# Low parts of the q, k, v and o weights: formed by an adding GpSimd DMA instead of a VectorE subtraction

## The chip, the core and the metric

The kernel runs on one core of a Trainium2 chip. A core has five engines with their own instruction queues: TensorE (PE, the matrix products; PEld is its weight load), VectorE (DVE), ScalarE (ACT), GpSimd (POOL) and SyncE (SP, which here only issues DMAs). Each queue runs in order and waits on semaphores for the others. Data move between HBM and SBUF by 16 DMA engines. The metric is the device time of one execution in microseconds (us).

## The reference

The program is a decoder trunk on 512 tokens of 1024 channels: a layer that mixes tokens by causal average pooling and a small linear map per group, a layer of causal stick-breaking attention with 16 heads of 64, and a squared-ReLU MLP with 4096 hidden channels behind each. All have an RMS norm in front and behind. What matters here is the attention layer:

```python
def rms_norm(x, g):
    y = xf * lax.rsqrt(jnp.mean(xf * xf, axis=-1, keepdims=True) + EPS)
    return (y * g.astype(jnp.float32)).astype(x.dtype)
...
kv = jnp.matmul(rms_norm(x, kv_norm_g), w_kv).reshape(B, S, 2, N_HEADS, HEAD_DIM)
...
q = jnp.matmul(h, w_q[j]).reshape(B, S, N_HEADS, HEAD_DIM).transpose(0, 2, 1, 3)
o = stick_breaking_attention(q, k, v)
m = jnp.matmul(o.transpose(0, 2, 1, 3).reshape(B, S, HD), w_o[j])
```

In the attention, the weight of a key is sigmoid(z) times the product of sigmoid(-z) over the keys between it and the query, and zero for keys from the query on.

## The kernel before, in words

Activations and weights are float32. A product is made of three TensorE products in the faster float32r form: an operand is split into a high part (the value rounded to float32r) and a low part (the value less its high part), and high x high, high x low and low x high are added up in PSUM. `up_block` (L534 to L536) and `mm3` (L209 to L211) issue these triples.

A weight block is 128 x 1024, 512 KB. `weight` (L105 to L121) makes its two parts. SyncE loads the block into a `raw` tile, of which there are two. For v, k and q `gains` scales it in place by a norm's gain on GpSimd, in two halves (L130). ScalarE casts it into the high part `hi` (L118). VectorE subtracts `hi` from `raw` into the low part `lo` (L120). For four blocks of the first MLP GpSimd makes the subtraction (`ON_POOL`). The parts lie in four tiles each, and `fill` and `get` make up to four weights ahead of their use, in the order of a list. There are 32 such blocks in the attention: eight each of v (four units of two halves), k and q (one a pair of heads) and o (the output projection).

The attention runs through a list of steps, `ATT_ORDER`. V makes the values of a unit of four heads, for the token tiles listed; P the queries and keys of a pair of heads; S its weights; T their transposes (L759); A their products with the values (L769); O and E the output projection. In S, TensorE makes the scores (L721, L722), ScalarE two sigmoids (L727, L728), GpSimd sets the part above the diagonal by affine selections (L733, eight a head), VectorE runs a product scan (L740) and a last product (L743). S0 to S7 below are the S steps of the pairs 0 to 7.

The program is not issued in the order in which it is written. A planner with its own cost of each instruction orders the engines' queues; the waits between engines follow from the tiles that are read and written. `issue_after` holds the scaling, cast and subtraction of a weight behind named instructions of the same engine (`behind`), so that they don't get ahead of the softmax. Within a queue nothing overtakes.

Of the kernel before, what the change touches and what calls it, by code (L numbers as in the profile page):

```python
# [10 lines left out]
F32 = mybir.dt.float32  # L11
F32R = mybir.dt.float32r
ACT = mybir.ActivationFunctionType
ALU = mybir.AluOpType

P = 128
# [16 lines left out]
# Columns of the score tile of a head: query tiles 3, 2, 1, 0, each with the keys it may see.  # L33
SEG = {3: (0, 512), 2: (512, 384), 1: (896, 256), 0: (1152, 128)}
NSEG = 1280
# The order of the pooling mixer: norm of a token tile (s), pooling (p), linear map and residual (m),
# norm (n), transposes (t); F: the next weights.
# [4 lines left out]
# Weights whose low part GpSimd makes, while VectorE has the norms to do.  # L42
ON_POOL = {("up", 0, j) for j in (0, 1, 2, 4)}

# The order of the attention. V: values of four heads, for the token tiles listed; K: keys of two
# heads for the first two token tiles; P: queries and keys of two heads; S: their weights; T: the
# transposes of those; A: their products with the values; O: output projection of four heads, for the
# token tiles listed; E: of the last eight.
# [6 lines left out]
# Rows of the gains that go along the free axis.  # L55
R_MIX_POST0, R_MLP_POST0, R_MIX_POST1, R_MLP_POST1, R_SCALE, R_MLP_PRE0, R_MLP_PRE1 = range(7)
# Blocks of the gains that go along partitions.
# [4 lines left out]
def trunk(ctx, tc, x, consts, gcol, grow, pw, wup, wdn, wq, wk, wv, wo, out):  # L62
# [18 lines left out]
    # ---- loads that everything waits for  # L81
# [19 lines left out]
    # The last instructions of a part by engine: the scaling and splitting of weights that are traced  # L101
    # after them keep behind them; from the first scores on (gate), behind all such work traced before.
    behind, latest = {}, {}

    # ---- weights: loaded, scaled by a gain if asked, split into two float32r parts  # L105
    def weight(src, tiles, scaled=None, on=nc.vector):
        raw = wts.tile([P, D], F32, tag="raw", bufs=2, name=name("raw"))
        nc.sync.dma_start(raw, src)

        def later(engine):  # L110
            return tc.issue_after(behind[engine].ins) if engine in behind else nullcontext()

        if scaled is not None:
            with later("pool"):
                scaled(raw)
        hi, lo = tiles
        with later("act"):
            nc.scalar.copy(hi, raw)  # L118
        with later("dve"):
            on.tensor_tensor(out=lo, in0=raw, in1=hi.bitcast(F32), op=ALU.subtract)  # L120
        return hi, lo  # L121

    def gains(lo, n):
        """scales the n blocks of a weight by the gains along partitions from column lo"""

        def scaled(raw):
            v = raw.rearrange("p (k c) -> p k c", k=n)
            g = gc[:, lo : lo + n].rearrange("p (k o) -> p k o", o=1)
            for h in (slice(0, n // 2), slice(n // 2, n)):
                nc.gpsimd.tensor_tensor(  # L130
                    out=v[:, h], in0=v[:, h], in1=g[:, h].broadcast_to((P, n // 2, D // n)), op=ALU.mult
                )

        return scaled
# [6 lines left out]
    def place(k):  # L141
        """hi and lo tiles of a weight"""
        if k[0] == "dn":
            return [dn_pool[0].tile([P, D], F32R, tag="w", bufs=8, name=name(x)) for x in "hl"]
        if k == ("o", 6):
            both = att_pool[0].tile([P, 2, D], F32R, tag="v", bufs=2, name=name("w"))
            return [both[:, 0], both[:, 1]]
        if k == ("o", 7):
            return [att_pool[0].tile([P, NSEG], F32R, tag="u", bufs=2, name=name(x))[:, :D] for x in "hl"]
        return [wts.tile([P, D], F32R, tag=f"w{x}", bufs=4, name=name(x)) for x in "hl"]  # L150

    def make():
        k, src, scaled = queue.pop(0)
        on = nc.gpsimd if k in ON_POOL else nc.vector
        made[k] = weight(src, place(k), scaled, on)
# [30 lines left out]
    # ---- parts of a layer  # L186
# [7 lines left out]
    def rstd(st, col, eps=EPS, op=ALU.add, third=False):  # L194
        """1 / rms from the mean squares of two halves in columns col and col + 1 (and of a third part,
        in column col + 4), and eps"""
        total = st[:, col + 2 : col + 3]
        latest["dve"] = nc.vector.tensor_scalar(
            out=total, in0=st[:, col : col + 1], scalar1=st[:, col + 1 : col + 2],
            scalar2=eps, op0=ALU.add, op1=op,  # L200
        )
        if third:
            nc.vector.tensor_tensor(out=total, in0=total, in1=st[:, col + 4 : col + 5], op=ALU.add)
        r = st[:, col + 3 : col + 4]
        latest["pool"] = nc.gpsimd.tensor_tensor(out=r, in0=total, in1=mhalf, op=ALU.pow)
        return r
# [9 lines left out]
    # ---- x += rms_norm(y) * gain, and the norm (with its gain, if given) and the transposes of the new  # L216
    # x, token tile by token tile, in steps that are traced where the engines get to them
# [3 lines left out]
    class Update:  # L221
        def __init__(self, t, gpost, scaled, eps=EPS, gpre=None, final=False):
            self.t, self.gpost, self.scaled, self.eps = t, gpost, scaled, eps
            self.gpre, self.final = gpre, final
            self.xn = xn_tile()
            self.st = keep.tile([P, 8], F32, tag=f"stat{t}", bufs=4, name=name("stat"))
            # The last tile of all ends in smaller parts, for less to do behind the last product.
            self.cuts = [NS[0], slice(512, 768), slice(768, 1024)] if final and t == T - 1 else NS

        def square(self, n, y, on):  # L230
            """part n of y, and its product with the gain"""
            cut = self.cuts[n]
            square_sum(y, self.xn[:, cut], self.st, (0, 1, 4)[n])
            on.tensor_tensor(out=self.scaled[:, cut], in0=y, in1=self.gpost[:, cut], op=ALU.mult)
# [18 lines left out]
        def rstd(self):  # L253
# [3 lines left out]
            # The MLP is homogeneous: f(c x) = c^2 f(x). It gets x / sqrt(m), m the mean square, and so  # L257
            # gives y (m + EPS) / m, whose norm has EPS ((m + EPS) / m)^2 in place of EPS. Thus no
            # token is small beside those that the MLP's products add it to. m is kept from 0.
# [33 lines left out]
    def contract(lhs, w, y, first, update=None, tiles=range(T), soon=False):  # L293
        """y[t] (+)= lhs.T @ w, token tile by token tile; update(t, y[t]) makes what follows each, the
        transposes of the first tile before the products of the last if soon"""
# [66 lines left out]
    class Seven:  # L362
        """y += r.T @ w over two pairs of blocks by the seven products of Strassen's algorithm in
        Winograd's form. The halves of the tokens (of r) and of the columns (of w) and the two blocks of
        a pair make the parts r11 ... w22; the products are summed over the pairs on TensorE:

            y11 = r11 w11 + r12 w21         y12 = u + s1 t1 + s4 w22
            y21 = u + s3 t3 + r22 t4        y22 = u + s1 t1 + s3 t3        u = r11 w11 + s2 t2
            s1 = r21 + r22    s2 = s1 - r11    s3 = r11 - r21    s4 = r12 - s2
            t1 = w12 - w11    t3 = w22 - w12   t2 = t3 + w11     t4 = w21 - t2  # L370

        A sum in PSUM is added to y whenever it is one of these sums, and then goes on."""

        # Bank pair, operands, and the part of y that gets what the bank pair holds by then.
# [12 lines left out]
        def feed(self, r):  # L387
            """the left operands that the next block of r brings"""
# [23 lines left out]
        def prepare(self):  # L412
            """the right operands one by one, in the order of their use"""
# [32 lines left out]
        def make(self, n):  # L446
            """the next n right operands"""
# [29 lines left out]
    def mlp(l, mp, update):  # L477
        """The last group of blocks goes plainly, token tile by token tile, as the update wants y."""
# [59 lines left out]
    # ---- layer 0: pooling mixer  # L538
    with tc.tile_pool(name="mix0", bufs=1, reuse_waits="tile") as mp:
        # Products that keep TensorE busy until the data are there: its clock is gated while it idles  # L540
# [87 lines left out]
    # ---- layer 0: MLP  # L628
# [5 lines left out]
    # ---- layer 1: stick-breaking attention  # L634
    with tc.tile_pool(name="att", bufs=1, reuse_waits="tile") as ap:
# [25 lines left out]
        def start(key):  # L661
            """the projection of the first two token tiles"""
# [19 lines left out]
        # The low parts of the keys of a head, above or below zeros.  # L682
# [27 lines left out]
        def weights(qk, a):  # L710
            """The weights of head a of a pair: sigmoid(z) times the product, over the keys between
            the key and the query, of sigmoid(-z); none for keys from the query on."""
# [110 lines left out]
    # ---- layer 1: MLP  # L823
# [6 lines left out]
def constants():  # L830
    """The identity, and the pooling windows as band matrices (source token, target token): of the
    first token tile, of a later one, and of a tile and the one before it."""
# [47 lines left out]
```

## Time and profile before

| | |
|---|---|
| median of 3 runs (range) | 999.75 us (999.0 to 1001.27) |
| span of the profiled execution | 999.6 us; the profile gives no other time of it |
| TensorE busy | 957.3 us, 96% |
| VectorE, ScalarE, GpSimd busy | 785.3, 555.7, 315.8 us |
| mean granted clock of TensorE | 0.984 |
| attention | about 350 to 650 us |

In the profile a group of instructions has the line of the kernel, the engine, the operation, the tiles (out<-in, buffer numbers left out), the shapes and the count, then the busy time and the mean duration of one, and last the idle time of the engine just before them and what ended it. In a table of windows each engine has its busy time and in brackets the number of its instructions. In a timeline a row has start and duration, and in square brackets the idle time before it.

### The profile page before, as it was taken

How to read it: one execution, taken by the hardware profiler on the slowest of the kernel's cores; microseconds unless marked ns; L12 is line 12 of the kernel's file. 1: busy time of each engine (PE TensorE's matmuls, PEld its weight loads, DVE VectorE, ACT ScalarE, POOL GpSimd, SP SyncE). 2: the span in 40 equal slices, each digit the busy share in tenths (PEclk: the TensorE clock that was granted, in tenths of full speed). 3: DMA queues.
4: the chain of work that ended last, by engine and by line, in shares of the span. 5: the costliest groups of instructions: out<-in, count | busy, mean ns of one | idle time of the engine just before them, and what ended most of it. 6: DMA issues, size and time to landing. Idle time of an engine off the chain costs nothing.

```text
span 999.6 us, 13220 instructions
## 1 busy us (share of the span) xinstructions
PE 957.3 (96%) x4823; PEld 812.1 (81%) x4823; DVE 785.3 (79%) x1115; ACT 555.7 (56%) x989; POOL 315.8 (32%) x351
## 2 busy tenths in 40 slices
PE   7898999999999999989998999989999999999997
PEld 6896888888888888888787988788888888888886
DVE  5987788878878747578687999989778878888636
ACT  5666646456455447556566666558556455464532
POOL 1732202112021156463475733436212021121103
PEclk8998999999999999999999999999999999999999
DMA  7253323323231330212121222244333233231102
GB/s 266 76 179 126 106 85 106 116 95 106 86 121 67 97 115 22 64 44 64 64 81 47 64 64 66 83 148 148 106 105 106 85 115 117 85 126 64 64 22 85
DMA packets 26993, 94.52 MB, mean 95 GB/s; under 512 B 3120, under 2 KB 3504, under 8 KB 26928
## 3 DMA queue, kind: packets, MB, share of 16 engines
q1 hardware_dynamic: 26928, 93.68, 28.3%
q8 instruction: 38, 0.62, 0.2%
q14 instruction: 27, 0.22, 0.1%
HBM read 91.57 MB, written 2.10 MB: 94 GB/s over the span
## 4 chain that ended last, share of the span: by engine, by line
PE 73%; DVE 9%; POOL 6%; ACT 5%; issue 4%; DMA 3%; SPq 0%; POOLq 0%; DVEq 0%; ACTq 0%
PE ps L456 26%; PE ps L536 12%; PE ps L535 12%; PE ps L534 12%; PE ps L209 2%; PE ps L210 2%; DVE l L120 2%; PE ps L211 2%; POOL w L733 1%; POOL u L733 1%; PE ps L769 1%; ACT h L118 1%; DMA xn<-in_wdn 1%; DVE x L240 1%; ACT xn L192 1%
## 5 line engine op out<-in xcount | busy, mean ns | idle before, releaser
L535 PE MATMUL ps<-xnl,h 128*128 128x512 f32 (+1 forms) x712 | 262.0, 369 | 4.1 <-DVE xnl L189 4.1
L536 PE MATMUL ps<-xnh,l 128*128 128x512 f32 (+1 forms) x712 | 262.1, 369 | 0.3 <-DVE l L120 0.3
L534 PE MATMUL ps<-xnh,h 128*128 128x512 f32 (+1 forms) x712 | 261.0, 369 | 0.0
L120 DVE TENSOR_TENSOR l<-raw,h 128x1024 fp32r<-128x1024 f32 x101 | 129.3, 1281 | 48.3 <-ACT h L118 47.8
L456 PE MATMUL ps<-w,s 128*128 128x512 f32 x672 | 164.3, 395 | 2.5 <-ACT s L188 2.1
L535 PEld LDWEIGHTS ps<-xnl,h 128*128 128x128 f32 x712 | 134.9, 190 | 26.1 <-DVE xnl L189 4.3
L456 PEld LDWEIGHTS ps<-w,s 128*128 128x128 f32 x672 | 127.4, 191 | 31.9 <-ACT s L188 3.0
L536 PEld LDWEIGHTS ps<-xnh,l 128*128 128x128 f32 x712 | 134.8, 189 | 22.7 <-DVE l L120 0.6
L534 PEld LDWEIGHTS ps<-xnh,h 128*128 128x128 f32 x712 | 134.2, 190 | 21.9 <-ACT xnh L188 0.2
L473 DVE TENSOR_TENSOR y<-ps,y 128x512 f32<-128x512 f32 x180 | 119.7, 685 | 40.5 <-PE ps L456 39.3
L118 ACT CAST h<-raw 128x1024 fp32r<-128x1024 f32 x105 | 110.3, 1053 | 61.4 <-PE ps L535 30.9
L404 POOL TENSOR_TENSOR s<-r,r 128x256 f32<-128x256 f32 x28 | 28.2, 1009 | 324.7 <-ACT r L490 324.7
L456 PE MATMUL ps<-w,r 128*128 128x512 f32 x504 | 123.8, 389 | 2.4 <-DVE r L189 2.4
L188 ACT CAST w<-t 128x512 fp32r<-128x512 f32 x112 | 69.1, 621 | 80.8 <-PE ps L456 61.1
L456 PEld LDWEIGHTS ps<-w,r 128*128 128x128 f32 x504 | 94.5, 188 | 22.4 <-DVE r L189 2.8
L130 POOL TENSOR_TENSOR raw<-raw,gc 128x512 f32<-128x512 f32 x48 | 61.0, 1291 | 91.1 <-DMA raw<-in_wv 53.3
L188 ACT CAST w<-xn 128x512 fp32r<-128x512 f32 x56 | 34.9, 623 | 90.3 <-PE ps L456 80.6
L189 DVE TENSOR_TENSOR w<-t,w 128x512 fp32r<-128x512 f32 x112 | 76.2, 702 | 0.7 <-ACT w L188 0.7
L740 DVE TENSOR_TENSOR_SCAN u<-u 128x512 f32<-128x512 f32 (+1 forms) x64 | 57.1, 913 | 13.6 <-POOL u L733 11.2
L188 ACT CAST s<-s 128x512 fp32r<-128x512 f32 x56 | 34.7, 621 | 45.8 <-POOL s L405 37.7
L189 DVE TENSOR_TENSOR s<-s,s 128x512 fp32r<-128x512 f32 x56 | 42.4, 762 | 22.1 <-ACT s L188 17.5
L403 POOL TENSOR_TENSOR s<-r 128x256 f32<-128x256 f32 x28 | 31.3, 1118 | 85.6 <-ACT r L490 72.2
(137 smaller groups left out, 1667.5 us busy)
## 6 DMA issues: line engine op xcount, KB each, us to landing
raw<-in_wup SPq DMA_DIRECT2D x64, 512.0 KB, 3.5
xn<-in_wdn SPq DMA_DIRECT2D x42, 512.0 KB, 3.6
spare<-in_wdn SPq DMA_DIRECT2D x14, 512.0 KB, 4.2
raw<-in_wdn SPq DMA_DIRECT2D x8, 512.0 KB, 3.4
raw<-in_wv SPq DMA_DIRECT2D x8, 512.0 KB, 3.5
raw<-in_wk SPq DMA_DIRECT2D x8, 512.0 KB, 3.5
raw<-in_wq SPq DMA_DIRECT2D x8, 512.0 KB, 3.5
raw<-in_wo SPq DMA_DIRECT2D x8, 512.0 KB, 3.5
```

The costliest lines, as they stand in the source:

```text
L118: nc.scalar.copy(hi, raw)
L120: on.tensor_tensor(out=lo, in0=raw, in1=hi.bitcast(F32), op=ALU.subtract)
L130: nc.gpsimd.tensor_tensor(out=v[:, h], in0=v[:, h], in1=g[:, h].broadcast_to((P, n // 2, D // n)), op=ALU.mult)
L188: latest["act"] = nc.scalar.copy(hi, src)
L189: latest["dve"] = nc.vector.tensor_tensor(out=lo, in0=src, in1=hi.bitcast(F32), op=ALU.subtract)
L403: nc.gpsimd.tensor_tensor(out=s3, in0=r1[:, lo], in1=r1[:, hi], op=ALU.subtract)
L456: nc.tensor.matmul(bank, r[:, a], w_[:, NS[b]], start=start and q == 0 and k == 0, stop=q == 1 and k == 2, skip_group_check=True,)
L473: nc.vector.tensor_tensor(out=part, in0=bank, in1=part, op=ALU.add)
L534: nc.tensor.matmul(pu[:, cols], wh[:, k, :], xnh[:, k, cols], start=k == 0, stop=False)
L535: nc.tensor.matmul(pu[:, cols], wh[:, k, :], xnl[:, k, cols], start=False, stop=False)
L536: nc.tensor.matmul(pu[:, cols], wl[:, k, :], xnh[:, k, cols], start=False, stop=k == KC - 1)
L740: nc.vector.tensor_tensor_scan(out=c, data0=c, data1=c, initial=1.0, op0=ALU.mult, op1=ALU.min)
```

## The change

For the q, k, v and o weights, VectorE's subtraction is left out. ScalarE writes the low tile with the negated block, rounded to float32r as the high part is, so that it holds minus the high part. Then a DMA issued from GpSimd's queue adds the raw block to it, from SBUF onto SBUF. The weights of both MLPs and of the pooling layer are made as before. The other lines of the diff take comments away.

```diff
+BY_DMA = ("q", "k", "v", "o")
...
         with later("act"):
             nc.scalar.copy(hi, raw)
+        if on is None:
+
+            with later("act"):
+                nc.scalar.mul(lo, raw, -1.0)
+            nc.gpsimd.dma_start(lo.bitcast(F32), raw, accum_op=ALU.add)
+            return hi, lo
         with later("dve"):
             on.tensor_tensor(out=lo, in0=raw, in1=hi.bitcast(F32), op=ALU.subtract)
         return hi, lo
...
         k, src, scaled = queue.pop(0)
-        on = nc.gpsimd if k in ON_POOL else nc.vector
+        on = nc.gpsimd if k in ON_POOL else None if k[0] in BY_DMA else nc.vector
         made[k] = weight(src, place(k), scaled, on)
```

The planner places the new instructions too, and so the order of the others in the attention moves a little on every engine but SyncE.

## The prediction

> **What bounds the kernel now.** I read the page from the top, then the table of windows for the attention, then the groups of lines on TensorE in that window, and last the order of time around single weights.
>
> ```profile
> span 999.6 us, 13220 instructions
> PE 957.3 (96%) x4823; PEld 812.1 (81%) x4823; DVE 785.3 (79%) x1115; ACT 555.7 (56%) x989; POOL 315.8 (32%) x351
> PE 73%; DVE 9%; POOL 6%; ACT 5%; issue 4%; DMA 3%; SPq 0%; POOLq 0%; DVEq 0%; ACTq 0%
> 350.00:650.00 300.00, 283.26 (x1592) 245.76 (x1592) 237.34 (x310) 183.63 (x358) 157.88 (x199) 0.99 0.20 64
> ```
>
> TensorE sets the time: busy for 957.3 of 999.6 us, and 73% of the chain that ended last. The change lies between about 350 and 650 us (last row, columns PE, PEld, DVE, ACT, POOL busy, then clock, DMA share and GB/s). There TensorE is idle for 300 - 283.3 = 16.7 us. This is the most that the stage can give back, and it holds only waits. What the change costs is any new wait of TensorE there.
>
> ```profile
> L759 PE MATMUL ps<-ident,w 128*128 128x128 f32 x160 | 21.2, 282 | 3.9 <-DVE w L743 3.2 <-DVE v L655 0.7
> L769 PE MATMUL ps<-ah,v 128*128 128x512 f32 (+3 forms) x64 | 19.8, 323 | 3.0 <-ACT ah L188 1.7 <-DVE v L655 0.7 <-DVE al L189 0.6
> L769 PE MATMUL ps<-al,v 128*128 128x256 f32 (+2 forms) x64 | 19.7, 335 | 2.3 <-DVE al L189 2.3
> L721 PE MATMUL ps<-k,q 128*128 128x512 f32 (+1 forms) x64 | 21.5, 351 | 2.0 <-DVE q L703 1.0 <-DVE v L655 1.0
> L209 PE MATMUL ps<-h,ohl 128*128 128x512 f32 x54 | 21.4, 396 | 1.8 <-DVE kl L694 1.1 <-DVE al L189 0.7
> L209 PE MATMUL ps<-h,xnh 128*128 128x256 f32 x128 | 37.0, 289 | 1.5 <-DVE kl L694 1.3 <-ACT xnh L188 0.2
> ```
>
> These are TensorE's groups of that window with the idle time before them. VectorE ended 3.9 + 1.3 + 2.3 + 2.0 + 1.8 + 1.3 = 12.6 us of it. So a shorter VectorE queue has at most about 12.6 us to win.
>
> **The change part by part.** It touches 32 weights, eight each of v, k, q and o.
>
> ```profile
> L120 DVE TENSOR_TENSOR l<-raw,h 128x1024 fp32r<-128x1024 f32 x101 | 129.3, 1281 | 48.3 <-ACT h L118 47.8
> L118 ACT CAST h<-raw 128x1024 fp32r<-128x1024 f32 x105 | 110.3, 1053 | 61.4 <-PE ps L535 30.9 <-PE ps L456 12.1 <-POOL raw L130 7.9
> raw<-in_wv SPq DMA_DIRECT2D x8, 512.0 KB, 3.5
> q1 hardware_dynamic: 26928, 93.68, 28.3%
> ```
>
> *Removed from VectorE:* 32 subtractions of 1.28 us are 41 us of its 237.3 busy us in the window. It is not the bound, so this is worth only what it takes from the 12.6 us. The ends are 0 (the same waits stand behind other work) and 12.6; I take half, 6.3, because each of those waits is for another VectorE instruction, before which only sometimes a subtraction stood.
>
> *Added to ScalarE:* 32 negations. The nearest row is the cast of the same tile, 1.05 us: 34 us, which takes ScalarE from 183.6 to about 217 of 300 us. It hides in ScalarE's idle time, 116 us; where there is none, each puts whatever follows it 1.05 us back. I count it once below, where two output weights follow each other.
>
> *Added to GpSimd and the DMA engines:* 32 transfers of 512 KB from SBUF onto SBUF with an addition. No such transfer is in the trace, nor any issued from GpSimd. The lower end for the time from the end of the negation to the landing is the load of a raw weight, 3.5 us. The data must be read twice. One packet takes 0.283 x 16 x 999.6 / 26928 = 0.168 us and an engine moves eight of them for 512 KB, so a second reading is 1.35 us and the transfer about 5 us; this I take, as it starts from the nearest row. As upper end I take twice that, 10 us, for an addition at half the pace and descriptors that GpSimd itself must write.
>
> The Trainium skill, "DMA: Bandwidth & Descriptors", section "Anatomy of one DMA — SWDGE (gpsimd) path", fits a DMA issued by GpSimd as about 2.0 us plus its bytes at 436 GB/s, which is an estimate of 3.2 us here; by that price the sum below would come to about 1007 us. The Trainium skill, "Collectives: The Full Stack", section "The bandwidth ceiling: the fold count and why AG ≠ RS ≠ AR", says that an adding transfer reads two sources and runs at half the pace for it, which goes with the longer value that I take.
>
> *Moved in order.* GpSimd's queue is in order and now holds, for each weight, the scaling, then the DMA, which waits there for ScalarE's negation, among the causal selections of the softmax (L733). In the changed program's order several of these DMAs stand behind a whole group of selections and behind the scaling of the next weight. SyncE's load of the next raw weight also waits, since there are two raw buffers and one now comes free only when the addition has landed. Before, both were VectorE's 1.2 us. So what counts is how early the low parts were. For most weights it was about 10 us ahead of TensorE, which hides 5 + 1.05 us less VectorE's 1.28. Six were tight, or become so by the queue.
>
> ```profile
> 429.57 1.03 POOL L733 TENSOR_SCALAR_AFFINE_SELECT w<-w 128x128 f32<-128x128 f32 x2
> 458.36 2.04 POOL L130 TENSOR_TENSOR raw<-raw,gc 128x512 f32<-128x512 f32 x2 [4.91 <-DMA raw<-in_wq]
> 434.52 0.41 PE L210 MATMUL ps<-l,xnh 128*128 128x256 f32 x1
> 445.88 0.40 PE L536 MATMUL ps<-xnh,l 128*128 128x512 f32 x1
> 452.41 1.04 POOL L733 TENSOR_SCALAR_AFFINE_SELECT w<-w 128x128 f32<-128x128 f32 x2
> 453.60 1.21 DVE L120 TENSOR_TENSOR l<-raw,h 128x1024 fp32r<-128x1024 f32 x1
> 454.86 0.50 PE L536 MATMUL ps<-xnh,l 128*128 128x512 f32 x1 [0.33 <-DVE l L120]
> 485.46 1.04 ACT L118 CAST h<-raw 128x1024 fp32r<-128x1024 f32 x1
> 486.54 1.23 DVE L120 TENSOR_TENSOR l<-raw,h 128x1024 fp32r<-128x1024 f32 x1 [0.25 <-ACT h L118]
> 487.82 0.50 PE L210 MATMUL ps<-l,ohl 128*128 128x512 f32 x1 [0.23 <-DVE l L120]
> 516.49 0.35 PE L210 MATMUL ps<-l,xnh 128*128 128x256 f32 x1
> 517.45 1.35 POOL L733 TENSOR_SCALAR_AFFINE_SELECT w<-w 128x128 f32<-128x128 f32 x2
> 518.84 1.49 DVE L743 TENSOR_TENSOR w<-w,u 128x1279 f32<-128x1279 f32 x1
> 520.75 2.13 PE L759 MATMUL ps<-ident,w 128*128 128x128 f32 x18
> 567.37 1.04 POOL L733 TENSOR_SCALAR_AFFINE_SELECT w<-w 128x128 f32<-128x128 f32 x2
> 571.75 0.28 PE L210 MATMUL ps<-l,xnh 128*128 128x256 f32 x1
> ```
>
> These are single rows in order of time: start, duration. With 5 us for a transfer:
> 1. First half of v, unit 1: its DMA now stands behind the selections of S0 (end 430.6) and a scaling (2.04): 432.6 + 5 = 437.6; TensorE wanted it at 434.5. Late by 3.1.
> 2. Keys of pair 2: their raw buffer comes free at 437.6; load 3.5, scaling 2.0, cast and negation 2.1, addition 5: 450.3, against 445.9 + 3.1. Late by 1.3.
> 3. Queries of pair 2: behind the selections of S1 (453.45, now 3.1 later) and a scaling: 458.6 + 5 = 463.6, against 454.9 + 4.4. Late by 4.3. Before, TensorE already waited here for the subtraction (0.33).
> 4. Second output weight: cast at 485.46, put back 1.05 by the negation of the first; cast, negation and addition end at 493.6, against 487.8. Late by 5.8.
> 5. Second half of v, unit 2: behind the selections of S3 (518.8) and a scaling: 520.8 + 5 = 525.8. The changed order has the transposes ahead of its use. TensorE comes to it at 516.5, does the first head's, waits about 1.5 for the second head's product (520.3), needs until 522.5, then waits 3.3. Together 4.8.
> 6. Second half of v, unit 3: behind the selections of S5 (568.4) and a scaling: 570.4 + 5 = 575.4, against 571.75. Late by 3.7.
>
> The sum is 3.1 + 1.3 + 4.3 + 5.8 + 4.8 + 3.7 = 23.0 us of new waiting, less 6.3 for VectorE: 16.7. The profiled execution spans 999.6 us, which is 0.15 below the median of the runs, 999.75, so both lead to 1016. With 3.5 us for a transfer the six are 1.6, 0, 4.1, 4.3, 3.3 and 2.2, in sum 15.5, and the time 1009, or 1002.5 if VectorE's 12.6 are won in full. With 10 us they are 8.1, 6.2, 4.4, 10.8, 9.8 and 8.7, in sum 48.0, and the time 1041, or 1048 if VectorE gives nothing.
>
> **The rivals.** *VectorE was what mattered (faster).* The planner that orders the changed program may have spread the work so that all six low parts land before their use; the DMAs are then hidden, and only VectorE's relief is left, in L743, L189 and L694, on which TensorE waits. Price: -6.3, 993.5 us; it ends below the old time as soon as the six together cost less than the relief, thus under 6.3 us. For it speaks that most weights were about 10 us early; against it that points 3 and 4 had no slack (0.33 and 0.23 us of waiting already) and that even 3.5 us makes the six 15.5.
>
> *The addition is dear.* If a transfer takes 10 us or more, or GpSimd is held while it issues, the selections come late too, and with them the transposes. At 10 us the time is 1041 to 1048. For it: nothing in the trace bounds an adding transfer from above. Against it: the DMA engines are 20% busy in the window, so 32 more transfers find room.
>
> *Hidden both ways.* New waits and relief cancel within 2 us, about 0.2%, which is also what a measurement of this kernel can tell from no change: 999.7 us. For it: 3.5 us with the full relief is only 2.9 above zero.
>
> That the change doesn't do what it says is no rival: the changed program has 32 fewer VectorE instructions, 32 more on ScalarE and 32 DMAs on GpSimd.
>
> **How the numbers follow.** The step-by-step case, a transfer between 3.5 and 7 us, has 0.64, with its own range 1003 to 1030. The dear addition has 0.18, the faster rival 0.12, the cancelling 0.06. So slower by over 0.2% has 0.82, faster 0.12, no change 0.06. The time is that of the first case, 1016. The range leaves out the faster rival and the upper part of the dear one: 1000 to 1044.
>
> **What would show it.** Right: waits of TensorE in L210 and L536 for the low part's DMA that are new and add up to 15 to 30 us between 430 and 650; GpSimd's scalings waiting longer for loads; landings of the new transfers near 5 us; VectorE's idle time up by about 40 us. Everything before 350 and after 660 should take as long as before. Wrong: landings of 10 us or more, selections that wait behind a DMA, or TensorE's idle time in the window unchanged or smaller. The prediction rests most on the 5 us and on the six places being in the order that I read.

## The result and the profile after

The changed kernel takes 1031.96 us, the median of four runs (1029.91 to 1034.8), against 999.97 us for the kernel before, the median of its four runs beside them. The ratio is 1.032, with a 95% interval of 1.0301 to 1.034: slower by 32 us. The prediction was 1016 us, with a range of 1000 to 1044, so the direction and the range held and the size was about half of what came. In the changed kernel's code, lines from the weight function on are 9 higher than before: the addition is L126, the negation L125, the cast L121, the scaling L139.

The head of the page, its shares of the chain that ended last, and the window that the prediction used, of the changed kernel:

```profile
span 1029.9 us, 13292 instructions
PE 965.7 (94%) x4823; PEld 817.5 (79%) x4823; DVE 755.6 (73%) x1083; ACT 585.2 (57%) x1021; POOL 329.4 (32%) x383
PE 31%; DVE 4%; DMA 2%; POOL 2%; ACT 2%; issue 1%; DVEq 0%; POOLq 0%; ACTq 0%; SPq 0%
350.00:650.00 300.00, 265.51 (x1466) 229.66 (x1466) 184.98 (x241) 195.11 (x354) 158.12 (x219) 0.95 0.44 108
```

TensorE is still the bound. Its busy time rose from 957.3 to 965.7 us, 8.4 us, and its idle time from 42.3 to 64.2 us, 21.9 us; together these are the 30.3 us of the span. In the window 350 to 650 us it was idle for 34.5 us, where it had been for 16.7.

The new transfers, in the table of DMA issues, the table of queues, and the table of waits (SyncE's own queue):

```profile
l<-raw POOLq DMA_DIRECT2D x31, 512.0 KB, 4.6
q1 hardware_dynamic: 26928, 93.68, 27.0%
q0 software_dynamic: 4608, 16.78, 8.5%
SPq L111 <- DMA l<-raw: 273.0, 31, 24.7
```

An addition of 512 KB lands 4.6 us after its issue. A packet of it takes 0.085 x 16 x 1029.9 / 4608 = 0.304 us, a packet of the other loads 0.270 x 16 x 1029.9 / 26928 = 0.165 us: nearly twice as long. SyncE, whose next load needs the raw buffer, waited for the additions 31 times, 273 us in all; this costs something only where the load is then late.

TensorE's groups with the most idle time before them, and GpSimd's two groups of weight work, in the view by line of the window 350 to 690 us (busy us, mean ns of one, then the idle time before them and what ended it):

```profile
L768 PE MATMUL ps<-ident,w 128*128 128x128 f32 x160 | 22.6, 291 | 10.2 <-DVE w L752 8.7 <-DVE q L712 1.5
L218 PE MATMUL ps<-h,xnh 128*128 128x256 f32 x128 | 38.7, 306 | 5.5 <-ACT h L121 3.4 <-ACT xnh L197 1.1 <-DVE kl L703 0.9
L219 PE MATMUL ps<-l,xnh 128*128 128x256 f32 x128 | 38.2, 299 | 3.2 <-DMA l<-raw 3.2
L219 PE MATMUL ps<-l,ohl 128*128 128x512 f32 x56 | 22.7, 406 | 1.5 <-DMA l<-raw 1.5
L139 POOL TENSOR_TENSOR raw<-raw,gc 128x512 f32<-128x512 f32 x47 | 54.2, 1197 | 47.6 <-DMA raw<-in_wv 16.3 <-DMA raw<-in_wk 15.2 <-DMA raw<-in_wq 14.3
L126 POOL DMA_DIRECT2D l<-raw x31 | 27.2, 876 | 68.2 <-ACT l L125 33.9 <-issue 28.3 <-PE ps L220 3.6
```

Only some 5 us of TensorE's idle time are put down to the low part's DMA itself. The largest wait, 10.2 us in front of the softmax's transposes (L768), is for VectorE's product (L752), and 3.4 us are for a cast of a weight. GpSimd's queue stood 68.2 us in front of the additions, 33.9 of them for ScalarE's negation and 28.3 in which the profile shows nothing that it waited for ("issue"), and issuing them took 27.2 us; the causal selections (L742) and scalings stand behind them in that queue. That this is what made the product and the cast late is not shown by these rows, and the small DMA below speaks against it.

Where the prediction named six places, these are the first products of the six low parts (timeline, TensorE: start, duration, then the wait):

```profile
440.14 0.58 PE L219 MATMUL ps<-l,xnh 128*128 128x256 f32 x1 [2.09 <-DMA l<-raw]
454.93 0.50 PE L545 MATMUL ps<-xnh,l 128*128 128x512 f32 x1 [0.37 <-DMA l<-raw]
469.04 0.80 PE L545 MATMUL ps<-xnh,l 128*128 128x512 f32 x1 [0.16 <-DMA l<-raw]
506.68 0.50 PE L219 MATMUL ps<-l,ohl 128*128 128x512 f32 x1 [1.02 <-DMA l<-raw]
541.07 0.39 PE L219 MATMUL ps<-l,xnh 128*128 128x256 f32 x1 [0.52 <-DMA l<-raw]
596.54 0.39 PE L219 MATMUL ps<-l,xnh 128*128 128x256 f32 x1 [0.62 <-DMA l<-raw]
687.14 0.39 PE L544 MATMUL ps<-xnl,h 128*128 128x256 f32 x1 [3.34 <-DVE xnl L198]
```

Against the rows of before in the prediction (434.52, 445.88, 454.86, 487.82, 516.49, 571.75) they come 5.6, 9.1, 14.2, 18.9, 24.6 and 24.8 us later. Each of the six waits for the DMA. But these delays are not waits alone. TensorE's busy time up to the sixth place, before and then after (view by windows: the stretch and its length, then busy time and number of instructions of TensorE, of its weight load, of VectorE, ScalarE and GpSimd, then clock, DMA share and GB/s), is

```profile
0.00:571.75 571.75, 545.43 (x2817) 465.24 (x2818) 443.28 (x620) 324.05 (x585) 205.57 (x238) 0.98 0.29 96
0.00:596.54 596.54, 550.65 (x2817) 468.00 (x2817) 420.56 (x595) 344.90 (x607) 211.51 (x261) 0.97 0.38 112
```

So TensorE had been idle for 26.3 us before and for 45.9 us after: of the 24.8 us, 19.6 are idle time and 5.2 are longer busy time for as many products. At the third, fourth and fifth place the new order had also put 9, 12 and 31 products ahead, by the count in the traces. The last of the seven rows is the first product of the MLP behind the attention. Its twin in the timeline of the kernel before is

```profile
657.02 0.38 PE L535 MATMUL ps<-xnl,h 128*128 128x256 f32 x1 [4.11 <-DVE xnl L189]
```

and so it is 30.1 us later: all of the loss lies in the attention.

### The profile page after: what moved, and what is told of

Read it like the earlier page. It is cut to its first block, busy times and chain, and to the rows that moved or that the text cites. A ratio compares the mean times of both kernels' runs of the same rounds, so it can differ in the third digit from the quotient of the medians.

```text
span 1029.9 us, 13292 instructions
## 1 busy us (share of the span) xinstructions
PE 965.7 (94%) x4823; PEld 817.5 (79%) x4823; DVE 755.6 (73%) x1083; ACT 585.2 (57%) x1021; POOL 329.4 (32%) x383
## 3 DMA queue, kind: packets, MB, share of 16 engines
q1 hardware_dynamic: 26928, 93.68, 27.0%
q0 software_dynamic: 4608, 16.78, 8.5%
## 5 line engine op out<-in xcount | busy, mean ns | idle before, releaser
L465 PE MATMUL ps<-w,s 128*128 128x512 f32 x672 | 161.2, 390 | 2.7 <-ACT s L197 1.8
L543 PEld LDWEIGHTS ps<-xnh,h 128*128 128x128 f32 x712 | 134.8, 190 | 24.8 <-DVE o L785 2.7
L121 ACT CAST h<-raw 128x1024 fp32r<-128x1024 f32 x105 | 110.3, 1051 | 76.5 <-PE ps L544 31.5
L129 DVE TENSOR_TENSOR l<-raw,h 128x1024 fp32r<-128x1024 f32 x70 | 88.8, 1268 | 34.3 <-ACT h L121 34.1
L749 DVE TENSOR_TENSOR_SCAN u<-u 128x512 f32<-128x512 f32 (+1 forms) x64 | 64.0, 1022 | 21.1 <-POOL u L742 18.9
L139 POOL TENSOR_TENSOR raw<-raw,gc 128x512 f32<-128x512 f32 x48 | 55.2, 1194 | 71.4 <-DMA raw<-in_wv 40.1
L198 DVE TENSOR_TENSOR w<-t,w 128x512 fp32r<-128x512 f32 x112 | 76.5, 706 | 0.6 <-ACT w L197 0.6
L198 DVE TENSOR_TENSOR r<-r,r 128x512 fp32r<-128x512 f32 (+1 forms) x60 | 46.8, 783 | 17.0 <-ACT r L197 16.9
L198 DVE TENSOR_TENSOR s<-s,s 128x512 fp32r<-128x512 f32 x56 | 42.5, 762 | 22.1 <-ACT s L197 17.5
```

The lines of the kernel that those rows point to most:

```text
L139: nc.gpsimd.tensor_tensor(out=v[:, h], in0=v[:, h], in1=g[:, h].broadcast_to((P, n // 2, D // n)), op=ALU.mult)
L198: latest["dve"] = nc.vector.tensor_tensor(out=lo, in0=src, in1=hi.bitcast(F32), op=ALU.subtract)
L465: nc.tensor.matmul(bank, r[:, a], w_[:, NS[b]], start=start and q == 0 and k == 0, stop=q == 1 and k == 2, skip_group_check=True,)
L543: nc.tensor.matmul(pu[:, cols], wh[:, k, :], xnh[:, k, cols], start=k == 0, stop=False)
L749: nc.vector.tensor_tensor_scan(out=c, data0=c, data1=c, initial=1.0, op0=ALU.mult, op1=ALU.min)
```

## The experiments

All were timed beside the kernel before, whose median was 1000.2 to 1002.1 us in the batches. The ratios are to it; one thousandth is about 1 us. One thing limits every comparison: the planner lays the instructions in an order of its own for each kernel. Only one experiment, the plain copy, has its instructions in the same order as the changed kernel on all five engines. Two more pairs come close: the small adding DMA on the kernel before has that kernel's order but for what GpSimd adds, and the one on the negation has that of the negation alone but for GpSimd's additions and eight places in VectorE's queue.

A whole time also holds what happens outside the attention. So the rows below that are called the stretch of the attention give the profiled execution of a kernel from the start of TensorE's 1701st product, near the end of the MLP in front, to the start of the first product of the MLP behind. They are of the view by windows, and the length less TensorE's busy time is its idle time.

**No low part at all.** This leaves out the low part for the 32 weights and shows what VectorE's relief is worth at most.

```diff
         if on is None:
-            with later("act"):
-                nc.scalar.mul(lo, raw, -1.0)
-            nc.gpsimd.dma_start(lo.bitcast(F32), raw, accum_op=ALU.add)
-            return hi, lo
+            return hi, hi
```

> The q, k, v and o weights get no low part at all (the high part is used in its place, so the low x high product is computed with wrong numbers; all products, loads and scalings stay). No subtraction, negation or adding DMA is left: this is VectorE's relief alone. Theory A (the relief is worth half of what VectorE made TensorE wait, as predicted): 999.97 - 6.3 = about 994 us. Theory B (the relief is worth nothing, since the waits come from VectorE's other work): 999 to 1001 us.

Measured: 988.39 us, ratio 0.9887 (0.9858 to 0.9915). The relief alone gains 11 us, and not the 6.3 that the prediction took. The stretch of the attention, before and then here, is

```profile
362.74:657.02 294.28, 273.43 (x1551) 237.50 (x1549) 238.16 (x312) 183.12 (x360) 153.96 (x197) 0.99 0.20 63
363.24:642.92 279.68, 268.10 (x1551) 234.39 (x1550) 198.38 (x281) 181.36 (x359) 147.50 (x196) 1.00 0.20 64
```

It is 14.6 us shorter. TensorE's idle time fell from 20.9 to 11.6 us, by 9.3, and its busy time by 5.3; 4.6 us were lost again in the MLP behind. So that 11 us lies close to the 12.6 us of waiting that VectorE ended is in part chance.

**The negation alone.** As the changed kernel, without the DMA.

```diff
             with later("act"):
                 nc.scalar.mul(lo, raw, -1.0)
-            nc.gpsimd.dma_start(lo.bitcast(F32), raw, accum_op=ALU.add)
             return hi, lo
```

> As e1_none, but ScalarE still writes the negated block into the low part (no DMA adds to it, so the low part is minus the high part). It adds ScalarE's 32 x 1.05 us to e1_none. Theory A (hidden in ScalarE's idle time): within 2 us of e1_none. Rival (ScalarE's queue sets the time): 5 us or more above e1_none.

Measured: 999.56 us over ten runs, ratio 0.9993 (0.9982 to 1.0005). With the negations all that the relief gained is gone, some 11 us, though ScalarE was 61% busy in the window before. The stretch of the attention is 14.3 us longer than without them:

```profile
359.73:653.66 293.93, 275.34 (x1551) 239.26 (x1550) 202.40 (x282) 208.88 (x389) 148.15 (x196) 0.97 0.20 63
```

Two rows of the waits in the window 350 to 650 us show where it may come from, first without and then with the negations (the line numbers differ by 2):

```profile
DVE v L661 <- ACT v L660: 8.4, 8, 2.2
DVE q L709 <- ACT q L708: 7.2, 8, 1.7
```

```profile
DVE v L663 <- ACT v L662: 13.0, 10, 2.5
DVE q L711 <- ACT q L710: 10.0, 8, 1.8
```

VectorE waits longer for ScalarE's casts of values and queries out of PSUM, which stand behind the negations in ScalarE's queue. The planner's order differs between the two kernels as well, so how much of the loss is the negations' alone is not shown.

**A small adding DMA, on the kernel before and on the negation alone.** GpSimd issues an adding DMA of 56 columns per weight onto a scratch tile that nobody reads; the first keeps VectorE's subtraction, the second has the negation and still no right low part. Both also add two such scratch tiles, which GpSimd clears at the start.

```diff
+            junk = junks.pop(0)
+            junks.append(junk)
+            nc.gpsimd.dma_start(junk, hi[:, :56].bitcast(F32), accum_op=ALU.add)
             return hi, lo
```

The second reads `lo[:, :56]` in place of `hi[:, :56]`.

> VectorE subtracts as before; GpSimd issues besides, for each of the 32 weights, an adding DMA of 56 columns of the high part onto a scratch tile that nobody reads. It has GpSimd's issue and its wait for ScalarE in GpSimd's queue, without a late low part and without holding the raw buffer. Theory A (the low part arrives late; the queue itself is hidden): up to 1003 us. Theory C (GpSimd's queue is held and the selections come late): 1010 us or more.

> As e2_neg (ScalarE negates, nobody subtracts, the low part is minus the high part), with an adding DMA of 56 columns of the low part onto a scratch tile issued from GpSimd, at the place where the changed kernel issues its own. VectorE relieved, ScalarE loaded, GpSimd's queue held and waiting for the negation; but the low part is not late and the raw buffer not held. Theory A (what is left of the 32 us is the late low part and the raw buffer): e2_neg's 999.6 plus the 7.6 of e3_junk, 1004 to 1011 us. Theory C (GpSimd's queue behind the negation is the main cost): 1020 us or more.

Measured: 1007.83 us, ratio 1.0073 (1.0052 to 1.0094), and 1008.01 us, ratio 1.0077 (1.0056 to 1.0097). These kernels are 7 to 8 us slower than their bases, but little of that lies where the small DMA is issued. The stretch of the attention, on the kernel before and then on the negation alone, is

```profile
362.33:657.67 295.34, 274.24 (x1552) 236.28 (x1550) 238.08 (x312) 182.89 (x360) 178.71 (x226) 0.98 0.24 66
363.87:658.51 294.64, 273.66 (x1552) 236.40 (x1550) 204.63 (x282) 208.84 (x389) 168.56 (x226) 0.98 0.25 66
```

It is 1.1 us longer than in the kernel before (294.28) and 0.7 us longer than with the negation alone (293.93). Yet the small DMA took as long to issue as the whole one, 27.0 us for 31, and GpSimd waited 40.8 us in front of it (view by line of the window 350 to 690 us, on the kernel before):

```profile
L128 POOL DMA_DIRECT2D junk<-h x31 | 27.0, 870 | 40.8 <-ACT h L121 40.3 <-DMA raw<-in_wk 0.4
```

A good part of the rest is slower products in the MLPs, at the full clock and without idle time. From 800 to 950 us, in the kernel before and then with the small DMA on it:

```profile
800.00:950.00 150.00, 150.00 (x664) 124.20 (x663) 119.24 (x170) 78.64 (x124) 27.19 (x30) 1.00 0.29 95
800.00:950.00 150.00, 150.00 (x658) 123.22 (x657) 119.59 (x169) 80.36 (x127) 28.60 (x31) 1.00 0.29 96
```

There are 658 products in place of 664, and from 100 to 350 us 1095 in place of 1104, though the first small DMA is issued only at 357.4 us. So these DMAs are not what slows the products. The scratch tiles are there from the start; no run has them alone, and the cause stays open. The place in GpSimd's queue, the wait for ScalarE there and the issue itself, is thus worth about 1 us in the attention, and not 7 to 8.

**A plain copy in place of the addition.** The same transfer without the addition, so that the low part is wrong.

```diff
-            nc.gpsimd.dma_start(lo.bitcast(F32), raw, accum_op=ALU.add)
+            nc.gpsimd.dma_start(lo.bitcast(F32), raw)
```

> The changed kernel with GpSimd's DMA as a plain copy of the raw weight, without the addition (the low part is then wrong: the weight itself). If the second read makes a transfer dearer by 1.35 us, landings near 3.3 us instead of 4.6, packets near 0.17 us instead of 0.304; the held raw buffer, the place in GpSimd's queue and ScalarE's negations stay, so 1022 to 1030 us. If the addition itself were the cause of the loss, near 1000 to 1010 us.

Measured: 1016.07 us, ratio 1.0145 (1.0119 to 1.017). The rows of this kernel, from the tables of DMA issues and queues and from the view of the line that issues it (least, median and largest duration in ns on GpSimd), and then that last row for the changed kernel:

```profile
l<-raw POOLq DMA_DIRECT2D x31, 512.0 KB, 3.1
q0 software_dynamic: 4608, 16.78, 4.3%
L126 POOL DMA_DIRECT2D l<-raw x31: 527/547/747, 357.3 to 645.2; - x31
```

```profile
L126 POOL DMA_DIRECT2D l<-raw x31: 850/863/1092, 354.7 to 654.2; - x31
```

With the same order of instructions, the addition alone makes the difference of about 16 us (17.5 thousandths by the ratios). It adds 1.5 us to each landing and 0.32 us to each issue on GpSimd; a packet of the copy takes 0.043 x 16 x 1016.8 / 4608 = 0.152 us, half of the addition's 0.304, which fits a second reading, though the trace doesn't show the readings themselves. The stretch of the attention, with the copy and then in the changed kernel, is

```profile
362.98:674.13 311.15, 282.94 (x1551) 244.39 (x1549) 203.32 (x282) 211.51 (x390) 167.98 (x228) 0.95 0.33 113
360.24:687.14 326.90, 284.89 (x1552) 244.75 (x1550) 211.57 (x282) 211.07 (x390) 170.74 (x228) 0.95 0.44 109
```

The addition makes it 15.8 us longer, 13.8 of them idle time. It is not the wait in GpSimd's queue that differs, for in front of the copies that is longer still, 73.8 us against 68.2 (view by line of the window 350 to 690 us):

```profile
L126 POOL DMA_DIRECT2D l<-raw x31 | 17.6, 566 | 73.8 <-ACT l L125 38.3 <-issue 23.5 <-PE ps L219 5.8
```

In that window GpSimd's selections (L742) were busy for 76.5 us with the copy and for 88.1 with the addition; why is not shown, and the profile's spans on GpSimd are rough. The result lies between the two expectations: the addition is neither the whole cause of the loss nor a small part of it.

**The addition from the high part.** The source of the adding DMA is the high tile, so that the low part becomes zero and the raw buffer is free after the negation.

```diff
-            nc.gpsimd.dma_start(lo.bitcast(F32), raw, accum_op=ALU.add)
+            nc.gpsimd.dma_start(lo.bitcast(F32), hi.bitcast(F32), accum_op=ALU.add)
```

> The changed kernel with the high part, not the raw block, as the source of the adding DMA, so that the low part becomes zero: the same DMA at the same place with the same lateness, but the raw buffer comes free after the negation and the next load does not wait for the landing. If the lateness of the low part alone makes the loss: 1026 to 1032 us. If the held raw buffer, which puts back the load, the scaling in GpSimd's queue and the selections behind it, makes most of it: 1008 to 1018 us.

Measured: 1010.27 us, ratio 1.0112 (1.0074 to 1.015): 22 us less than the changed kernel (three runs lay at 1008 to 1012 us, one at 1019.85), though its additions took longer to land:

```profile
l<-h POOLq DMA_DIRECT2D x31, 512.0 KB, 6.1
```

This looked like proof that the raw buffer, held until the landing, was the larger part. But the planner had also moved the scalings ahead, so two things had changed. The next pair was to separate them.

**A third raw buffer, and its control.** Every third of the 32 weights gets a raw buffer of its own; the room comes from four instead of five buffers for the transposed softmax parts, which the control has alone.

```diff
-        raw = wts.tile([P, D], F32, tag="raw", bufs=2, name=name("raw"))
+        count[0] += on is None
+        if on is None and att_pool[0] is not None and count[0] % 3 == 0:
+            raw = att_pool[0].tile([P, D], F32, tag="raw3", name=name("raw"))
+        else:
+            raw = wts.tile([P, D], F32, tag="raw", bufs=2, name=name("raw"))
...
-                hi = ap.tile([P, S], F32R, tag="ah", bufs=5, name=name("ah"))
-                lo = ap.tile([P, S], F32R, tag="al", bufs=5, name=name("al"))
+                hi = ap.tile([P, S], F32R, tag="ah", bufs=4, name=name("ah"))
+                lo = ap.tile([P, S], F32R, tag="al", bufs=4, name=name("al"))
```

> The changed kernel with a third raw buffer in the attention (every third of the 32 weights takes it); the room for it comes from four instead of five buffers for the transposed softmax parts. To be compared with e12_ctrl, which has the four buffers alone. If the raw buffer that is held until the addition lands is the largest part of the loss (21.7 us between e7_hisrc and the changed kernel), the load of the next weight can now start one weight earlier: 10 to 20 us below e12_ctrl, 1012 to 1022 us, and SyncE's wait for the adding DMAs (273 us before) falls under 100. If the loss is in GpSimd's queue itself, within 3 us of e12_ctrl.

> The changed kernel with four instead of five buffers for the transposed softmax parts (ah, al): the control of e11_raw3. If these buffers have slack, 1032 us like the changed kernel; if they are short, some us above it.

Measured: 1046.23 us with the third buffer, ratio 1.044 (1.0409 to 1.0472), and 1040.99 us for the control, ratio 1.0404 (1.0372 to 1.0436). The third buffer gained nothing, and my theory that the held buffer was the largest part lost its support, though here too the planner's orders differ. The buffers did come free earlier. The key weight of the fourth pair shows it in the two timelines, first with the third buffer (its scaling, a cast of keys and, behind it, the cast of the weight), then in the control:

```profile
451.95 2.04 POOL L143 TENSOR_TENSOR raw<-raw,gc 128x512 f32<-128x512 f32 x2 [4.64 <-DMA raw<-in_wk]
470.27 0.58 ACT L706 CAST k<-ps 64x512 fp32r<-64x512 f32 x1
470.76 1.04 ACT L125 CAST h<-raw 128x1024 fp32r<-128x1024 f32 x1
```

```profile
462.30 2.24 POOL L139 TENSOR_TENSOR raw<-raw,gc 128x512 f32<-128x512 f32 x2
468.37 0.58 ACT L702 CAST k<-ps 64x512 fp32r<-64x512 f32 x1
468.86 1.04 ACT L121 CAST h<-raw 128x1024 fp32r<-128x1024 f32 x1
```

The raw block is scaled 10 us sooner, and then lies there: its cast comes no sooner, because the kernel puts the casts and splits of weights behind the last work of the part on ScalarE (here the casts of the keys). The low part starts from that cast, whatever the raw buffer does, and the longer way from the cast to the landing is paid each time. SyncE's wait did not fall to under 100 us either, as I had expected, but was

```profile
SPq L115 <- DMA l<-raw: 285.0, 30, 22.1
```

So SyncE's long wait for the additions is no measure of the loss. The control shows that the four buffers themselves cost about 8 us: they had no slack in the changed kernel.

**The small DMA holding the raw buffer.** As the first small DMA, on the kernel before, but reading the raw block.

```diff
-            nc.gpsimd.dma_start(junk, hi[:, :56].bitcast(F32), accum_op=ALU.add)
+            nc.gpsimd.dma_start(junk, raw[:, :56], accum_op=ALU.add)
```

> The kernel before, with the small adding DMA of e3_junk (56 columns of a weight onto a scratch tile) reading the raw weight instead of the high part; e3_junk gave 1007.8 us. If holding the raw buffer until a DMA in GpSimd's queue has landed costs time by itself, 1012 us or more, though less than in the changed kernel, since VectorE's subtraction holds the same buffer too. If not, 1007 to 1009 us.

Measured: 1010.42 us, ratio 1.0088 (1.0063 to 1.0112), against 1.0073 (1.0052 to 1.0094) before. This falls between the two expectations, and the intervals overlap; by these the hold costs 1 or 2 us here, if anything. In the profiled executions the stretch of the attention is 300.3 us against 295.3, in another order, so its price is not settled.

**The copy from SyncE.** VectorE subtracts in the raw block in place, and SyncE copies it into the low tile with a plain DMA.

```diff
+            with later("dve"):
+                nc.vector.tensor_tensor(out=raw, in0=raw, in1=hi.bitcast(F32), op=ALU.subtract)
+            nc.sync.dma_start(lo.bitcast(F32), raw)
             return hi, lo
```

> VectorE subtracts into the raw tile in place, and SyncE, not GpSimd, moves the result to the low part with a plain 512 KB DMA. It has the later low part (about 3.5 us) and the raw buffer held until the DMA has landed, but nothing of it in GpSimd's queue, and VectorE is not relieved; SyncE's queue holds it between the loads instead. Theory A (lateness and the raw buffer): 1010 to 1020 us. Theory C (GpSimd's queue is what costs): 1000 to 1006 us.

Measured: 1014.12 us, ratio 1.0148 (1.0126 to 1.0171). So a transfer on the way from the cast to the low part costs 14 us even where neither GpSimd nor ScalarE nor an addition is in it. But this copy also stands between the loads in SyncE's queue and holds the raw buffer, and how much of the 14 us comes from that is not shown.

**The output weights alone.** `BY_DMA = ("o",)`: eight of the 32 weights.

> The changed kernel with the adding DMA for the eight output weights alone; v, k and q as before. Of the six places of the prediction only the fourth (5.8 us) is left, and of ScalarE's extra 34 us a quarter. Theory A (the places add up): 1004 to 1009 us. Rival (a quarter of the weights, a quarter of the loss): 1008 us as well, so this run tells of place 4 by its trace; rival (the output weights, which GpSimd does not scale, cost nothing): 998 to 1001 us.

Measured: 1007.08 us, ratio 1.006 (1.004 to 1.008). A quarter of the weights costs about a fifth of the loss, though these need no scaling by GpSimd. The prediction's fourth place is in its trace: that product starts at 494.31 us, after 2.49 us of waiting for the DMA, and so 6.5 us later than before (5.8 was predicted); 12 more products ran ahead of it.

**Subtractions on GpSimd.** The kernel before, with twelve low parts subtracted by GpSimd, to use VectorE's relief without a DMA.

```diff
+ON_POOL |= {("o", c) for c in (0, 2, 3, 4, 5, 6, 7)} | {("k", 3), ("q", 3), ("k", 6), ("k", 7), ("q", 7)}
...
-        with later("dve"):
+        with later("pool" if on is nc.gpsimd else "dve"):
```

> The kernel before, with twelve of the 32 low parts (output weights 0 and 2 to 7, keys 3, 6, 7, queries 3, 7) subtracted by GpSimd in stretches where its queue is idle, and neither ScalarE's work nor a DMA added. If VectorE's relief is worth what e1_none showed (11.8 us for 32) and costs nothing elsewhere, 12 of 32 give 4.4: 995 to 996 us. If GpSimd's longer subtraction (2.67 us against 1.28) makes low parts or selections late: 1000 us or more.

Measured: 1001.91 us over twelve runs, ratio 1.0011 (1.0001 to 1.0021): no gain. No kernel here that computes the whole is faster than the kernel before.

## Why the prediction was right in direction and short in size

Read as a chain, the medians go: before 1000, without the low part 988.4, with ScalarE's negations 999.6, with a full plain copy 1016.1, with the addition 1032.0. The steps are -11.6, +11.2, +16.5 and +15.9. In the stretch of the attention they are -14.6, +14.3, +17.2 and +15.8. Only the last compares equal orders; the others include what the planner made of them. Of the third, the place in GpSimd's queue is about 1 us, by the small DMA; the rest comes with the full transfer, by which the low part is late and the raw buffer held, and these two were not parted.

- *Removed from VectorE, -6.3 taken out of 0 to 12.6.* Under-sized: 11 us by the kernel without a low part, and 9.3 us of idle time in the stretch of the attention. The reason given for the half, that only sometimes a subtraction stood before the instruction waited for, was not tried by itself.
- *Added to ScalarE, "34 us" that "hides in ScalarE's idle time, 116 us".* This step failed. The negation took what the cast did (1.06 us), but with the negations, and the order that came with them, all that the relief had gained was lost. VectorE's waits for the casts behind them grew, so the idle time was not where it was needed. The prediction had counted 1.05 us.
- *The transfer, "about 5 us".* Right: 4.6, as 3.1 for a copy and 1.5 more for the addition (1.35 was predicted, for a second reading). The Trainium skill, "DMA: Bandwidth & Descriptors", section "Anatomy of one DMA — SWDGE (gpsimd) path", by which I had estimated 3.2 us, agrees with the plain copy's 3.1 and not with the addition's 4.6. The Trainium skill, "Collectives: The Full Stack", section "The bandwidth ceiling: the fold count and why AG ≠ RS ≠ AR", which has half the pace for an adding transfer, agrees with the packets, 0.304 against 0.152 us.
- *The six late low parts, 23.0 in sum.* Right in place: at each of them TensorE waits for the DMA. The prediction's running sums were 3.1, 4.4, 8.7, 14.5, 19.3 and 23.0; the six products came 5.6, 9.1, 14.2, 18.9, 24.6 and 24.8 us later. That the last two numbers lie so close is in part luck: of the 24.8 us, 5.2 are longer busy time, which is in no term of the sum, and 19.6 are idle time, and at three places the order had changed. How much of VectorE's relief is in the 19.6 can't be told from it.
- *Nothing behind the sixth place.* This failed: another 30.1 - 24.8 = 5.3 us came between 597 and 687 us, at the later weights of the attention and the norm behind it; 2.2 of them are idle time.
- *"What the change costs is any new wait of TensorE there."* This failed. Of the 30.3 us of span, 21.9 are idle time, against 16.7 predicted, and 8.4 are longer busy time for the same products, which the sum put at nothing.
- *New waits "in L210 and L536 for the low part's DMA" of 15 to 30 us.* Wrong in form. They are some 5 us; the rest appears as waits for the softmax's product, a cast or a split that had come late in turn.
- *The dear addition.* A part of this rival came true: no landing took 10 us (the longest took 6.7), but GpSimd was held 0.88 us for each issue and the selections did come late: VectorE waited 18.9 us for them in the window 350 to 690 us, and 11.2 before. The prediction gave GpSimd's issue no price of its own; by the small DMA, which is issued as slowly, that price is about 1 us, so by that run the issue is not what makes the addition dear.
- *The other signs.* The time from the first product of the MLP behind to the end stayed, as predicted: 342.6 us before and 342.8 after. GpSimd's scalings did not wait longer for their loads: 47.6 us of idle time stood before them, and 91.1 before the change.

From 16.7 to 30.3 us of span: 5.2 us more of idle time and 8.4 us of busy time. The working of the transfer's length was also too soft: it gave 23.0 - 15.5 = 7.5 us for 1.5 us more per landing, where the plain copy shows about 16 us for 1.5 us and the 0.32 us of issue.

Two things stay open: how 1.5 us more for each landing become 16 us, and the addition from the high part, 22 us faster than the changed kernel. The third buffer speaks against the held raw buffer as its cause by itself. The order that the planner laid for it, with scalings ahead of the selections, is what remains; that was argued, and no run had that order with the raw block as source.

## What to carry to other kernels

Price work that is moved to an engine by what queues behind it there at that moment, not by the engine's idle time in a window: 34 us of ScalarE's work "in 116 us of idle time" went with a loss of 11 us. A DMA between two steps that follow each other closely costs at every place that had less slack than its latency. Read an experiment in the stage that it is meant to change: the small DMA's kernels lost 7 to 8 us in all, and about 1 us in the attention. To test whether a buffer is short, give one more: a long wait in the queue of loads (273 us here) proves nothing.

## What the hardware showed beside that

TensorE's busy time grew by 8.4 us with the same 4823 products. The mean granted clock fell from 0.984 to 0.977. If the clock is either full or half, as nearly all records have it, the time at half is twice the rest: 2 x 0.016 x 999.6 = 32 us before and 2 x 0.023 x 1029.9 = 47 us after. These stretches begin behind short idle times. Of the changed kernel, TensorE's last product before one of them and its next (timeline), and then windows (the clock is the third column from the right):

```profile
429.19 1.25 PE L768 MATMUL ps<-ident,w 128*128 128x128 f32 x10
434.88 1.54 PE L768 MATMUL ps<-ident,w 128*128 128x128 f32 x6 [4.44 <-DVE w L752]
```

```profile
432.00:432.50 0.50, 0.00 (x0) 0.00 (x0) 0.38 (x2) 0.00 (x0) 0.50 (x3) 1.00 0.00 0
432.50:433.00 0.50, 0.00 (x0) 0.00 (x0) 0.49 (x1) 0.00 (x0) 0.50 (x1) 0.73 0.00 0
434.00:437.00 3.00, 2.12 (x10) 2.00 (x10) 1.76 (x3) 1.54 (x3) 2.53 (x2) 0.50 0.00 0
440.00:443.00 3.00, 2.86 (x13) 2.87 (x14) 2.94 (x6) 2.02 (x5) 0.00 (x0) 0.51 0.95 156
443.00:446.00 3.00, 3.00 (x24) 2.91 (x23) 0.55 (x1) 0.00 (x0) 0.14 (x1) 1.00 0.82 229
```

The last product ends at 430.44. The clock falls to half at about 432.73, since 0.27 of the half microsecond up to 433 is missing at a step of one half (0.27 x 0.5 / 0.5 = 0.27 us), so 2.3 us after TensorE went idle, and it stays there for some 10 us, through the next gap. The Trainium skill, "TensorE: Matmul & The Clock Gate", section "What's actually happening", says that the clock is halved after an idle window of about 3.4 us; the trace agrees in the halving, and here it came after the shorter time. The 2.3 us is no threshold, though: all changes of the clock in this trace's records lie whole multiples of 3.41 us apart, and in the 3.41 us up to 432.73 TensorE was still busy for 1.1 us. The 47 - 32 = 15 us more at half the clock can take up to 7.5 us of work, so by this estimate they can make most of the 8.4 us. The plain copy has the same busy time as the changed kernel, 965.7 us, so over the whole, longer busy time is not what the addition adds. That idle time causes the halving was not tried.

A DMA that adds holds GpSimd longer while it is issued than one that copies, 0.863 against 0.547 us in the median, for the same 512 KB. The small adding one of 56 columns, 28 KB, holds it as long, 0.862 us.
